# A fused two-block transformer forward on one core: a fourth weight slot in attention, another order in the last expert unit, unread products in three waits

## The chip, the cores and the metric

The kernel runs on one core of a Trainium2 chip. The metric is the device time of one execution in microseconds. The engines are named as in the profile: PE is TensorE (matmul), PEld its weight loads, DVE VectorE, ACT ScalarE, POOL GpSimd, and SP is the engine whose queue issues most of the DMA transfers. SBUF is the on-chip memory, and PSUM the small memory of eight banks into which TensorE writes. A bank holds 512 fp32 columns on 128 partitions.

## The reference

The sequence has 256 tokens, the model 1024 channels, and everything is fp32. The first block is one layer, cut here to what matters:

```
mod = silu(c) @ w_ada + b_ada                  # shifts, scales, gates
h   = rms_norm(x) * (1 + sc_mix) + sh_mix
u, v, tq, tk, tv, nq, nk, nv, ga, gb = split(h @ w_in + b_in)
o_a = u * (w_s applied to layer_norm(v) + tiny_attention(tq, tk, tv) @ tiny_w_o)
o_b = neighbourhood_attention(nq, nk, nv, context, rpb)       # 16 heads of 32
x   = x + g_mix * ((sigmoid(ga)*(o_a @ w_up_a) + sigmoid(gb)*(o_b @ w_up_b)) @ w_out)
h2  = rms_norm(x) * (1 + sc_ffn) + sh_ffn
y   = shared_swiglu(h2) + sum over the top 8 of 64 experts of weight * swiglu_e(h2)
x   = rms_norm(x + g_ffn * y) * final_norm_g
```

The second block is two layers of stick-breaking and block attention with gates, a SwiGLU feed-forward part and layer norms, on the first block's x. Weights are some 400 MB, which are read once.

## The kernel before

**Weights.** They are streamed as chunks of 128x2048 fp32 (1 MB) in one fixed order by the class `Ring`. `Ring.open(pool, n, limit)` gives it n slots of a pool; `_issue` asks for the next chunk by a DMA on SP (L222) or, where its number is in `halves`, by two DMAs of half a chunk. `done(i)` gives the slot of chunk i to the next chunk of the order. An expert's source is a function, since the expert's number is read at run time.

**Products.** Most products keep fp32 accuracy by a split: ACT casts a weight chunk to `whi` (L352), DVE subtracts to get `wlo` (L353), and TensorE makes three products in a fast fp32 format (L392 to L394). The split of a chunk is made ahead, into one of two buffers. Some small products are in full fp32, which TensorE does by two instructions each.

**Order of the work.** Instructions are put in order on each engine by a planner that simulates their times and takes the order in which they are written as priority; a semaphore is set wherever one engine reads what another wrote. `follow()` and `issue_after` hold TensorE to a written order.

**Start.** Each of the six parts of `mod` is made by `ada_group(g)`: products of silu(c) with chunks of w_ada (L701), then `end()` adds the bias (`row`, L708), then `fm()` transposes `row` (L714) and DVE copies it to `mod` (L719). The first group stands ahead of the modulated input `xT` (L844), its cast `hh` (L288) and rest `hl` (L289), which are the operands of the first in-projection.

**Attention stage** (183 to 279 us in the trace). `weave` mixes two lists: the main one has the in-projection chunks of the two gates (ga, gb), each chunk split and multiplied, with further w_ada chunks consumed by DVE between them (`gate`, L749); the other has eight steps of the spatial gating unit (`sgu`, L1245 to L1250) and the neighbourhood attention (`na`). The ring has three slots here. In `na`, for each of four head groups and two halves of the queries, TensorE makes scores (L1311), DVE adds the bias table T, ACT takes the exponentials P (L1265), TensorE transposes them (L1278), ACT copies them to a tile PT (L1279), and `av` multiplies by the values (L1344) and by the reciprocal of the sums: DVE takes the reciprocal of four sums per row, spread to 32 columns each (`rB`, L1335), TensorE transposes that (L1337), ACT copies it (`o`, L1340). PT has two buffers; the gating unit's constants (`tw`) lie in one of them.

**Experts.** Experts sit in 26 units of one, two or four experts which share 128 rows; the last unit has four, with 32 rows each. For a unit TensorE gathers its tokens, multiplies by gate and up (L1627), ACT and DVE form the activation, TensorE transposes it to `aT` (L1656), and `down(p, h)` multiplies by the down chunks for each half h of the output columns: for f in two halves of the inner dimension, for e in the experts, with expert e in column tile e of the array (L1666). DVE multiplies by the gate (`yf`, L1763), ACT and DVE split the result into `yh` and `yl` (L1764, L1765), and `comb` adds it to the tokens' sums by four products for each of the two (L1679).

**Final.** `a(t)` makes the sums of squares (ACT, L1879) and the normed `xr` (DVE, L1885); `b` transposes it (L1931) and splits it for the second block.

Of the kernel before, what the change touches and what calls it, by code (L numbers as in the profile page):

```python
# [9 lines left out]
F32 = mybir.dt.float32  # L10
# [4 lines left out]
OP = mybir.AluOpType  # L15
# [6 lines left out]
SLOT = 2048  # L22
# [10 lines left out]
UNITS = [(2, 0), (2, 2), (2, 4), (2, 6)]  # L33
# [146 lines left out]
class Ring:  # L180
# [29 lines left out]
    def _issue(self, pool):  # L210
        if pool.name in self.lasting and self.wait_from <= self.next < self.wait_to:

            self.held.append(pool)
        elif self.next < self.limit[pool.name]:
            t = pool.tile([128, SLOT], F32, tag="w", name="w")
            src = self.src[self.next]
            if self.next in self.halves:
                for h in range(2):
                    s = slice(h * SLOT // 2, (h + 1) * SLOT // 2)
                    self.nc.sync.dma_start(t[:, s], src[:, s])  # L220
            else:
                self.last = self.nc.sync.dma_start(t[:], src() if callable(src) else src)  # L222
            self.tiles[self.next] = t
            self.home[self.next] = pool
            self.next += 1
            if self.next == self.stop:
                self.wait_from, self.wait_to = self.stop + self.EARLY, math.inf
                self.free()
# [43 lines left out]
class Kernel:  # L272
# [38 lines left out]
    @contextmanager  # L311
    def follow(self):

        traced = self.nc.cur_bb.bb.instructions
        n = len(traced)
        with self.tc.issue_after(self.pe_last) if self.pe_last else ExitStack():
            yield
        for i in traced[n:]:
            if i.engine == mybir.EngineType.PE:
                self.pe_last = i  # L320

    def last(self, engine):
        return next(i for i in reversed(self.nc.cur_bb.bb.instructions) if i.engine == engine)
# [244 lines left out]
    def program(self):  # L568
        tc, nc, A = self.tc, self.nc, self.A
        with ExitStack() as es:  # L570
# [66 lines left out]
            self.ring.add(order)  # L637
            self.ring.stop = self.ring.wait_to = self.i_2[0][0]
            self.ring.wait_from = self.ring.stop - self.KEEP
            self.ring.halves = (self.i_ada[3], self.i_uv[0])  # L640
            self.setup()
            self.block1()
            self.block2()
# [46 lines left out]
    def ada_group(self, g):  # L690
        nc = self.nc
        st = {}

        def begin():
            st["ps"] = self.accp.tile([128, 512], F32, tag="acc", name="acc")

        def step(k):
            i = self.i_ada[4 * g + k // 2]
            w = self.ring.get(i)[:].rearrange("p (k c) -> p k c", k=2)
            for j in range(4):  # L700
                nc.tensor.matmul(st["ps"][32 * j:32 * j + 32, 0:256], self.silp[:, k, :], w[:, k % 2, j * 256:(j + 1) * 256],  # L701
                                 start=k == 0, stop=k == 7, tile_position=(0, 32 * j))
            if k % 2:
                self.ring.done(i)

        def end():
            row = self.prep.tile([128, 256], F32, tag="row", name="row")
            nc.vector.tensor_tensor(row[:], st["ps"][:, 0:256], self.bada[:, g], op=OP.add)  # L708
            st["row"] = row

        def fm():
            pt = self.accp.tile([128, 512], F32, tag="acc", name="acc")
            for h in range(2):
                nc.tensor.transpose(pt[:, h * 128:(h + 1) * 128], st["row"][:, h * 128:(h + 1) * 128], self.ident)  # L714
            src = pt[:, 0:256].rearrange("p (h j c) -> p h j c", h=2, c=32)
            for n in range(2):
                dst = self.mod[:, n, 4 * g:4 * g + 4].rearrange("p (j h) r -> p h j r", h=2)
                for r in range(2):
                    nc.vector.tensor_copy(dst[:, :, :, r], src[:, :, 2 * n:2 * n + 2, r])  # L719
            ks = slice(4 * g, 4 * g + 4)  # L720
            for r in range(2):
                nc.vector.scalar_tensor_tensor(self.a1[:, r, ks], self.mod[:, 1, ks, r], 1.0, self.vecs[:, V_NMG + 4 * g:V_NMG + 4 * g + 4],
                                               op0=OP.add, op1=OP.mult)

        return [begin] + [lambda k=k: step(k) for k in range(8)] + [end, fm]
# [56 lines left out]
    def block1(self):  # L782
# [227 lines left out]


        tmp, tmp_es = self.pool("atmp", "right", bufs=2)
        oah = op.tile([128, 8, 256], F32R, name="oah")
        oal = Parts()
        obh = op.tile([128, 4, 256], F32R, name="obh")
# [13 lines left out]
        self.weave(main, bg)  # L1029
        self.dump("oa", oah[:].bitcast(F32))  # L1030
        self.dump("ob", obh[:].bitcast(F32))
        tmp_es.close()
        att_es.close()
        xp, xp_es = self.pool("xp", "right")
# [196 lines left out]

    def sgu(self, tmp, tT, u, vn, oah, oal):
        nc, A = self.nc, self.A
        big = tmp.tile([128, 2048], F32, tag="PT", name="tw")
        two, bs, wst = big[0:64, 0:1024], big[64:65, 0:1024], big[:, 1024:2048]
        nc.sync.dma_start(two, A["two"])
        nc.sync.dma_start(bs, A["bs"])
        nc.sync.dma_start(wst, A["wst"])
        ones1 = self.ones[64:65, :]

        def sgu(g):
            ps = self.accp.tile([128, 512], F32, tag="acc", name="acc")
            o = ps[:, 0:256]
            gs = slice(g * 128, (g + 1) * 128)
            nc.tensor.matmul(o, two[:, gs], tT[:], start=True, stop=False, skip_group_check=True)  # L1245
            nc.tensor.matmul(o, ones1, bs[:, None, gs].to_broadcast([1, 2, 128]), start=False, stop=False, skip_group_check=True)
            for n in range(2):
                nc.tensor.matmul(ps[:, n * 128:(n + 1) * 128], vn[:, n, gs], wst[:, gs], start=False, stop=n == 1,
                                 skip_group_check=True)
            nc.vector.tensor_tensor(o, u[g][:], o, op=OP.mult)  # L1250
            u[g] = None
            lo = self.up.tile([128, 256], F32R, tag="u", name="oal", bufs=9)
            oal.parts.append(lo)
            self.split(o, oah[:, g], lo[:])

        return [lambda g=g: sgu(g) for g in range(8)]
# [24 lines left out]
    def na(self, ap, tmp, qd, kd, nv, obh, obl):  # L1281
        nc, A, c = self.nc, self.A, self.c
        st = {}
# [40 lines left out]

        def trp(g, q, j):
            if j == 0:
                st["PT", g, q] = tmp.tile([128, 4, 4, 128], F32, tag="PT", name="PT")
            self.transposeP(st.pop(("p", g, q, j)), st["PT", g, q][:, :, j, :], 4)

        def av(g, q):  # L1330
# [1 line left out]
            r = st.pop(("r", g, q))  # L1332
            ps = self.accp.tile([128, 512], F32, tag="acc", name="acc")
            rB = tmp.tile([128, 4, 32], F32, tag="obf", name="rB")
            nc.vector.reciprocal(rB[:], r[:, :, None].to_broadcast([128, 4, 32]))  # L1335

            nc.tensor.matmul(ps[:, 128:256], rB[:].rearrange("p a b -> p (a b)"), self.ident, start=True, stop=False,  # L1337
                             skip_group_check=True)
# [214 lines left out]
    def moe(self, xnh, xnl, gf, h2, after, mmes, ranks, overflow):  # L1553
# [97 lines left out]
        def tra(p):  # L1651
# [4 lines left out]
            nc.vector.tensor_copy(aT[:], ps[:, 0:256])  # L1656
            st["aT"] = aT

        def down(p, h):
            y = self.bank(pg, "y")  # L1660
            n = UNITS[p][0]
# [84 lines left out]
            nc.gpsimd.dma_start(t[:], bass.AP(tensor=r.tensor, offset=r.offset + R_FG + h * 512, ap=[[0, 128], [1, 512]]))  # L1746
            self.fg.append(t)
        comb(nu - 2)
        down(nu - 1, 0)
        down(nu - 1, 1)  # L1750
        comb(nu - 1)
        self.overflow_loop(pg, xnh, xnl, [xgs[0][:].rearrange("p a b -> p (a b)"), wx[0][:], wx[1][:], xgs[1][:, :, 0:64]], gf)
        self.ring.go_on()
        mp_es.close()
# [105 lines left out]
    def final(self, fp):  # L1860
# [29 lines left out]

        a(0)
        a(1)
        self.pieces = 4
        b(0)
        self.open_hlx(0)
# [505 lines left out]
```

## Time and profile before

| | |
|---|---|
| median of 3 runs | 1612.58 us (1611.51 to 1612.89) |
| the profiled execution's own time | 1612.77 us |
| its span | 1611.0 us |
| mean granted clock of TensorE | 0.99 |
| TensorE, DVE, ACT busy | 97%, 55%, 39% of the span |
| instructions | 26016 |

The span goes from the first to the last instruction; the rest of the own time lies around it. A busy share is of the whole span; the stages differ, so the rows below are taken stretch by stretch. The granted clock is in parts of full speed: 1.00 is 2.4 GHz and 0.50 is 1.2 GHz. In rows of waits the instruction that waited is named first, then the one that it waited for.

### The profile page before, as it was taken

What the parts mean: (1) busy time and instruction counts of PE and PEld (TensorE: products, weight loads), DVE (VectorE), ACT (ScalarE), POOL (GpSimd) and SP (SyncE); (2) the same over time, 40 slices, a digit from 0 to 9 for tenths busy, and PEclk for the clock granted to TensorE, in tenths of its full rate; (3) what the DMA queues carried; (4) which work ended last, traced back from release to release, by engine and by line L of the source; (5) the groups of instructions that cost most, each with busy time, mean ns of one, the idle gap of its engine ahead of it and who ended that gap; (6) DMA issues with size and microseconds to landing.
All of it is one profiled execution on the core that took longest, in us unless ns stands there. A gap on an engine that the chain in (4) does not pass through costs nothing. (4 is left out here: it accounts for less than half of the span.)

```text
span 1611.0 us, 26016 instructions
## 1 busy us (share of the span) xinstructions
PE 1557.7 (97%) x10509; PEld 1204.2 (75%) x10509; DVE 878.6 (55%) x1639; ACT 632.3 (39%) x1171; POOL 12.8 (1%) x23
## 2 busy tenths in 40 slices
PE   6999988999999999999989999999999999999997
PEld 4799876975443444443349999899999999899996
DVE  3696697663332323332344667964446565975453
ACT  3633366442111111111134756554433656644440
POOL 0000000000000000000000000000000000000000
PEclk9999999999999999999999999999999999999999
DMA  9788586878999999999955446565552444756530
GB/s 369 267 312 273 154 229 196 332 296 343 397 421 420 421 420 421 421 420 420 422 231 191 154 139 213 199 235 185 184 181 79 157 158 137 250 215 209 184 131 27
DMA packets 62972, 419.48 MB, mean 260 GB/s; under 512 B 7393, under 2 KB 9057, under 8 KB 14210
## 3 DMA queue, kind: packets, MB, share of 16 engines
q1 hardware_dynamic: 59010, 408.63, 67.7%
q0 software_dynamic: 1088, 5.61, 1.0%
q10 hardware_dynamic: 2752, 3.55, 0.6%
q8 instruction: 83, 1.36, 0.3%
q14 instruction: 39, 0.32, 0.1%
HBM read 413.05 MB, written 4.19 MB: 259 GB/s over the span
## 5 line engine op out<-in xcount | busy, mean ns | idle before, releaser
L353 DVE TENSOR_TENSOR wlo<-w,whi 128x1024 fp32r<-128x1024 f32 (+1 forms) x384 | 374.9, 1014 | 171.2 <-ACT whi L352 168.7
L352 ACT CAST whi<-w 128x1024 fp32r<-128x1024 f32 (+1 forms) x384 | 319.2, 883 | 316.9 <-PE mm L393 140.1
L392 PE MATMUL mm<-xTh,whi 128*128 128x256 f32 x960 | 274.5, 286 | 0.0
L394 PE MATMUL mm<-xTh,wlo 128*128 128x256 f32 x960 | 271.5, 283 | 0.0
L393 PE MATMUL mm<-xTl,whi 128*128 128x256 f32 x960 | 271.0, 282 | 0.0
L1627 PE MATMUL gu<-w,xg 128*64 128x512 f32 (+2 forms) x936 | 207.0, 596 | 0.0
L392 PEld LDWEIGHTS mm<-xTh,whi 128*128 128x128 f32 x960 | 182.9, 191 | 2.2 <-issue 1.4
L393 PEld LDWEIGHTS mm<-xTl,whi 128*128 128x128 f32 x960 | 183.4, 191 | 0.6
L394 PEld LDWEIGHTS mm<-xTh,wlo 128*128 128x128 f32 x960 | 182.8, 190 | 0.0
L1627 PEld LDWEIGHTS gu<-w,xg 128*64 128x64 f32 (+2 forms) x936 | 58.7, 127 | 98.5 <-issue 93.7
L1666 PE MATMUL y<-w,aT 128*64 128x512 f32 (+2 forms) x432 | 114.4, 599 | 0.0
L1648 DVE SCALAR_TENSOR_TENSOR sil<-sil,wsl,gu 128x256 f32<-128x256 f32 x26 | 12.5, 481 | 128.2 <-ACT sil L1647 127.6
L1764 ACT CAST yh<-yf 128x512 fp32r<-128x512 f32 x52 | 32.2, 619 | 125.9 <-DVE yf L1763 125.9
L392 PE MATMUL mm<-hh,whi 128*128 128x256 f32 x256 | 76.1, 299 | 5.6 <-ACT whi L352 3.9
L1763 DVE TENSOR_TENSOR yf<-y,gf 128x512 f32<-128x512 f32 x52 | 35.9, 690 | 79.4 <-PE y L1666 79.4
L394 PE MATMUL mm<-hh,wlo 128*128 128x256 f32 x256 | 75.0, 295 | 2.9 <-DVE wlo L353 2.9
L1666 PEld LDWEIGHTS y<-w,aT 128*64 128x64 f32 (+2 forms) x432 | 32.7, 126 | 57.5 <-issue 55.4
L393 PE MATMUL mm<-hl,whi 128*128 128x256 f32 x256 | 74.9, 294 | 0.3 <-DVE hl L289 0.3
L484 PE MATMUL acc<-whi,xTh 128*128 128x256 f32 x256 | 73.8, 289 | 0.0
L485 PE MATMUL acc<-wlo,xTh 128*128 128x256 f32 x256 | 72.6, 285 | 0.0
L486 PE MATMUL acc<-whi,xTl 128*128 128x256 f32 x256 | 72.4, 286 | 0.1
L1647 ACT ACTIVATE sil<-gu 128x256 f32<-128x256 f32 x26 | 10.0, 383 | 134.3 <-PE gu L1627 134.3
(449 smaller groups left out, 3119.9 us busy)
## 6 DMA issues: line engine op xcount, KB each, us to landing
w<-in_we SPq DMA_DIRECT2D x171, 1024.0 KB, 19.8
w<-in_w SPq DMA_DIRECT2D x156, 1024.0 KB, 4.9
w<-in_wada SPq DMA_DIRECT2D x23, 1024.0 KB, 8.9
wx<-in_we SPq DMA_DIRECT2D x21, 1024.0 KB, 19.8
ks<-kd SPq DMA_DIRECT2D x8, 512.0 KB, 7.3
lngb<-in_rows POOLq DMA_DIRECT2D x4, 1024.0 KB, 5.2
T<-in_rpb SPq DMA_DIRECT2D x8, 384.0 KB, 7.9
qs<-qd SPq DMA_DIRECT2D x16, 128.0 KB, 8.3
```

What stands on the lines that cost most here:

```text
L352: nc.scalar.copy(hi[:, s], w[:, s])
L353: self.lo_of[i] = nc.vector.tensor_tensor(lo[:, s], w[:, s], hi[:, s].bitcast(F32), op=OP.subtract)
L392: nc.tensor.matmul(ps, hi[:, k, mm], h, start=first, stop=False, skip_group_check=True)
L393: nc.tensor.matmul(ps, hi[:, k, mm], l, start=False, stop=False, skip_group_check=True)
L394: nc.tensor.matmul(ps, lo[:, k, mm], h, start=False, stop=last, skip_group_check=True)
L484: nc.tensor.matmul(o, h, wh, start=k == 0 and c % 2 == 0, stop=False, skip_group_check=True)
L485: nc.tensor.matmul(o, h, wl, start=False, stop=False, skip_group_check=True)
L486: nc.tensor.matmul(o, l, wh, start=False, stop=k == 7 and c % 2 == 1, skip_group_check=True)
L1627: nc.tensor.matmul(st["gu"][m * e:m * e + m, :], xg[:, k, s0:s0 + m], w[:, k % 4, :], start=k == 0, stop=k == 7, tile_position=(0, m * e))
L1666: nc.tensor.matmul(y[m * e:m * e + m, :], st["aT"][:, f * 128 + e * m:f * 128 + e * m + m], w[:, f, h * 512:(h + 1) * 512], start=f == 0, ...
L1763: nc.vector.tensor_tensor(t[0:n], y[0:n], g[0:n, h * 512:(h + 1) * 512], op=OP.mult)
L1764: nc.scalar.copy(yh[0:n], t[0:n])
```

## The change

In five parts, as in the diff:

1. `Ring._issue` can load a chunk whose source is a function by two halves, and the last down chunk of the last expert unit is added to `halves`.
2. `idle(ps, n)` makes n products of the identity with itself that nobody reads. Four are put behind the last product of the first ada group (columns 256 to 383 of the bank that `row` reads), seven behind its transposes (the same columns of the bank that `mod` reads), and one plus twelve between `a` and `b` of the final norm, into a bank of their own.
3. The attention stage gets a pool `extn` of one weight slot, opened at its start and closed at its end. The tiles with tag PT (`tw` and PT) have one buffer instead of two.
4. In `av`, DVE takes the reciprocal of the four sums in place and then copies it to the 128x128 tile.
5. For the last expert unit `down_last` takes the products expert by expert (for e, for f, for h; chained in that order), keeps `yf` whole in fp32, and `comb_last` adds it by four full fp32 products instead of eight in the fast format.

```diff
-            if self.next in self.halves:
+            if self.next in self.halves and not callable(src):
...
+            elif self.next in self.halves:
+                src = src()
                 for h in range(2):
                     s = slice(h * SLOT // 2, (h + 1) * SLOT // 2)
                     self.nc.sync.dma_start(t[:, s], src[:, s])
...
+    def idle(self, ps, n):
+        for _ in range(n):
+            self.nc.tensor.matmul(ps, self.ident, self.ident, start=False, stop=False, skip_group_check=True)
...
-            self.ring.halves = (self.i_ada[3], self.i_uv[0])
+            self.ring.halves = (self.i_ada[3], self.i_uv[0], self.i_d[-1][-1])
...
         def end():
+            if g == 0:
+                with self.tc.issue_after(self.last(mybir.EngineType.PE)):
+                    self.idle(st["ps"][:, 256:384], 4)
...
+            if g == 0:
+                with self.tc.issue_after(self.last(mybir.EngineType.PE)):
+                    self.idle(pt[:, 256:384], 7)
...
         tmp, tmp_es = self.pool("atmp", "right", bufs=2)
+        extn, extn_es = self.pool("extn", "right")
+        self.ring.open(extn, 1, self.i_upa[0])
...
+        extn_es.close()
         tmp_es.close()
...
-        big = tmp.tile([128, 2048], F32, tag="PT", name="tw")
+        big = tmp.tile([128, 2048], F32, tag="PT", name="tw", bufs=1)
...
-                st["PT", g, q] = tmp.tile([128, 4, 4, 128], F32, tag="PT", name="PT")
+                st["PT", g, q] = tmp.tile([128, 4, 4, 128], F32, tag="PT", name="PT", bufs=1)
...
-            nc.vector.reciprocal(rB[:], r[:, :, None].to_broadcast([128, 4, 32]))
+            nc.vector.reciprocal(r[:], r[:])
+            nc.vector.tensor_copy(rB[:], r[:, :, None].to_broadcast([128, 4, 32]))
...
+        def down_last(p):
+            n = UNITS[p][0]
+            m = 128 // n
+            ys = [self.bank(pg, "y") for _ in range(2)]
+            for e in range(n):
+                w = self.ring.get(self.i_d[p][e])[:].rearrange("p (k c) -> p k c", k=2)
+                for f in range(2):
+                    for h in range(2):
+                        with self.follow():
+                            nc.tensor.matmul(ys[h][m * e:m * e + m, :], st["aT"][:, f * 128 + e * m:f * 128 + e * m + m],
+                                             w[:, f, h * 512:(h + 1) * 512], start=f == 0, stop=f == 1, tile_position=(0, m * e))
+            for i in self.i_d[p]:
+                self.ring.done(i)
+            for h in range(2):
+                t = self.xp.tile([128, 512], F32, tag="x1%d" % h, name="yf")
+                nc.vector.tensor_tensor(t[:], ys[h][:], gf[:, h * 512:(h + 1) * 512], op=OP.mult)
+                st["y", p, h] = t
+
+        def comb_last(p):
+            ST = st.pop(("ST", p))[0]
+            ys = [st.pop(("y", p, h)) for h in range(2)]
+            for t in range(2):
+                for h in range(2):
+                    nc.tensor.matmul(self.acc[t][h][:], ST[:, t * 128:(t + 1) * 128].bitcast(F32), ys[h][:],
+                                     start=False, stop=False, skip_group_check=True)
...
         comb(nu - 2)
-        down(nu - 1, 0)
-        down(nu - 1, 1)
-        comb(nu - 1)
+        self.pe_last = None
+        down_last(nu - 1)
+        comb_last(nu - 1)
...
         a(0)
         a(1)
+        ps = self.mmp.tile([128, 512], F32, tag="mm", name="mm")
+        nc.tensor.matmul(ps[:, 0:128], self.ident, self.ident, start=True, stop=False, skip_group_check=True)
+        self.idle(ps[:, 0:128], 12)
```

## Rows read from the trace of the kernel before

**Rows 1.** The page: span, and busy time (share of the span) xinstructions by engine.
```profile
span 1611.0 us, 26016 instructions
...
PE 1557.7 (97%) x10509; PEld 1204.2 (75%) x10509; DVE 878.6 (55%) x1639; ACT 632.3 (39%) x1171; POOL 12.8 (1%) x23
```

**Rows 2.** Windows: stretch, length, busy PE PEld DVE ACT POOL, granted clock, DMA, GB/s.
```profile
21.55:28.38 6.83, 5.84 (x25) 5.55 (x26) 6.83 (x16) 4.58 (x10) 0.00 (x0) 0.50 1.02 420
45.00:50.00 5.00, 4.89 (x28) 4.17 (x28) 4.56 (x15) 3.58 (x9) 0.00 (x0) 1.00 0.00 0
171.70:175.10 3.40, 3.40 (x17) 1.99 (x15) 2.27 (x4) 2.94 (x5) 0.00 (x0) 1.00 0.95 206
175.00:182.00 7.00, 7.00 (x25) 5.13 (x24) 3.65 (x7) 0.95 (x3) 0.00 (x0) 0.51 0.46 159
183.00:279.00 96.00, 83.44 (x741) 71.24 (x739) 83.52 (x117) 61.47 (x139) 2.77 (x5) 0.96 0.63 185
745.20:748.60 3.40, 3.40 (x16) 0.78 (x16) 0.48 (x1) 0.38 (x1) 0.00 (x0) 1.00 1.01 422
837.30:840.70 3.40, 3.28 (x16) 2.98 (x15) 3.40 (x11) 3.40 (x10) 0.00 (x0) 0.50 0.00 0
```

**Rows 3.** Waits of TensorE, 183 to 279 us: total, times, longest.
```profile
PE mm L392 <- ACT whi L352: 3.4, 2, 1.9
PE mm L394 <- DVE wlo L353: 1.9, 3, 0.8
```

**Rows 4.** Waits of TensorE, 835 us to the end, the two largest.
```profile
PE mm L1931 <- DVE xr L1885: 4.4, 1, 4.4
PE acc L2247 <- DVE qkT L2157: 0.4, 2, 0.2
```

**Rows 5.** Timeline at the start: begin, duration, engine, line [idle before it <- releaser].
```profile
19.70 0.42 DVE L708 TENSOR_TENSOR row<-acc,bada 128x256 f32<-128x256 f32 x1 [8.70 <-DMA w<-in_w]
...
20.72 0.37 DVE L719 COPY mod<-acc 128x4 f32<-128x4 f32 x4 [0.59 <-PE acc L714]
...
22.23 0.79 PE L392 MATMUL mm<-hh,whi 128*128 128x256 f32 x2 [1.55 <-ACT hh L288]
```

**Rows 6.** Timeline: fp32 products of 128 columns one after the other.
```profile
163.47 1.50 PE L1248 MATMUL acc<-tw,v 128*128 128x128 f32 x12
```

**Rows 7.** Line L1344: its products (ns least, median, most), and a wait.
```profile
L1344 PE MATMUL acc<-PT,nv x256: 272/273/298, 200.6 to 281.0; 128*32 128x128 f32 x128
...
  ACT o L1340: 1.6, 5
```

**Rows 8.** Waits of SP's queue, 183 to 279 us.
```profile
SPq L222 <- DVE gate L749: 19.9, 4, 7.5
```

**Rows 9.** Groups by line, 183 to 279 us: busy us, mean ns | idle before.
```profile
L1279 ACT COPY PT<-acc 128x512 f32<-128x512 f32 x32 | 18.3, 589 | 12.6 <-PE acc L1278 12.6
...
L1335 DVE RECIPROCAL rB<-rs 128x128 f32<-128x128 f32 x8 | 7.5, 942 | 1.2 <-ACT P L1265 1.2
```

**Rows 10.** Timeline: two small operations of DVE.
```profile
7.82 0.16 DVE L306 TENSOR_TENSOR rs_w<-rs_y 128x2 f32<-128x2 f32 x1
...
68.32 0.22 DVE L687 CAST ub<-cst 128x128 bf16<-128x128 f32 x1
```

**Rows 11.** Timeline: the down products of two units with four experts, and what follows.
```profile
745.89 1.90 PE L1666 MATMUL y<-w,aT 128*32 128x512 f32 x4
...
821.81 0.42 DVE L1656 COPY aT<-misc 128x256 f32<-128x256 f32 x1
...
823.07 1.04 PE L1666 MATMUL y<-w,aT 128*32 128x512 f32 x2
...
...
824.71 3.67 PE L1666 MATMUL y<-w,aT 128*32 128x512 f32 x30
...
828.42 0.69 DVE L1763 TENSOR_TENSOR yf<-y,gf 128x512 f32<-128x512 f32 x1 [0.18 <-PE y L1666]
...
830.79 0.63 PE L1679 MATMUL acc<-yl,ST 128*128 128x512 f32 x2
```

More of the change, by code (lines that the diff above doesn't have):

```diff
@@ L216, in _issue @@
             src = self.src[self.next]
-            if self.next in self.halves:
+            if self.next in self.halves and not callable(src):
+                for h in range(2):
+                    s = slice(h * SLOT // 2, (h + 1) * SLOT // 2)
+                    self.nc.sync.dma_start(t[:, s], src[:, s])
+            elif self.next in self.halves:
+                src = src()
                 for h in range(2):
@@ L1657, in tra @@
             st["aT"] = aT
+        def down_last(p):
[19 more added lines that the diff above has]
+            for t in range(2):
+                for h in range(2):
+                    nc.tensor.matmul(self.acc[t][h][:], ST[:, t * 128:(t + 1) * 128].bitcast(F32), ys[h][:],
+                                     start=False, stop=False, skip_group_check=True)
         def down(p, h):
```

## Prediction

> **What bounds the kernel now.** I read the page first, then the table of windows, the waits of TensorE (PE) stretch by stretch, the groups by line where an engine is full, and the timeline at the three places that are edited. The page gives a span of 1611.0 us with TensorE busy in 97% of it and VectorE (DVE) in 55% [rows 1], so in the mean a microsecond comes off only where TensorE has less to do or waits less. The edits lie in four stretches, and each has its own limit.
>
> At the start, from 21.55 to 28.38 us, DVE is busy in all 6.83 us, the DMA engines are full, and TensorE is granted 0.50, which is 1.2 GHz of its two levels 1.2 and 2.4 [rows 2]. Later, from 45 to 50 us, the DMA stands at 0.00 while TensorE is busy in 4.89 of 5: the transfers wait for slots there, so what is lost or won before 45 us stays. In the attention stage, 183 to 279 us, TensorE has 83.44 and DVE 83.52 busy in 96 us at a mean clock of 0.96, and the DMA is at 0.63 [rows 2]. So neither bandwidth nor one engine alone is the limit; the two engines wait for each other. The waits of TensorE there begin with 3.4 us on whi and 1.9 on wlo, the split halves of the next weight chunk [rows 3]. Behind 835 us the waits of TensorE are one of 4.4 us (the final norm) and next to it 0.4 [rows 4]: the second block is bound by TensorE, so a shift at 835 us reaches the end whole.
>
> **The change part by part.** All is counted on the profiled execution, 1612.77 us (1611.0 of span and 1.77 around it), which lies 0.19 above the median of the runs shown, 1612.58.
>
> *Unread products at the start.* Four go between the last product of the first ada group and the DVE addition `row` (L708), seven between the transposes and the copies `mod` (L719) [rows 5]. A product in full fp32 is two instructions; twelve of them with 128 columns take 1.50 us [rows 6], 0.125 each. So 8 × 0.125 = 1.0 us stand before `row` and 14 × 0.125 = 1.75 before `mod`, if the readers wait for them. They write columns 256 to 383 of a bank of which only columns 0 to 255 are read, but the trace has this case: L1344 writes columns 0 to 127 of a bank and waited five times, 1.6 us in all, for ACT's copy `o`, which reads columns 128 to 255 of it [rows 7]. So I take it that they wait. `row` to `hh` is a chain (row, transposes, mod, a, xT, hh): it ends in the 1.55 us that TensorE waits for `hh` [rows 5], and DVE has no gap behind it [rows 2], so at worst the whole 2.75 us come out late. Against that, TensorE would stay at 2.4 GHz in the 6.83 us of half clock and could regain up to half of them, 3.4. The ends are 2.75 − 3.4 = −0.65 and +2.75. I take about the middle, +1.1: the lower end would need a DVE with time to spare, the upper a clock that TensorE could make no use of.
> The Trainium skill (PSUM — Partial Sum Buffer, "PSUM bank collisions raise a hardware error") says that accesses of two engines to PSUM are to be kept apart by bank and quadrant of partitions, not by address. L1344's waits agree with it; by this rule the products delay their readers (the sum above), and by a rule of addresses this term would be −0.65 and the total 1.75 lower.
>
> *The fourth slot.* SP waits with ring transfers for DVE's ada step `gate` (L749), 19.9 us in four, up to 7.5 [rows 8]: the next but one chunk is asked for only when a slot comes free in the midst of the chunk before it, so it lands late, its split comes late, and TensorE waits for whi. With one more slot the transfer is asked for a chunk earlier. What goes is the 3.4 us on whi; beyond them at most the 1.9 on wlo, and what the two spells of low clock cost, (1 − 0.96) × 96 = 3.8 us. I take −3.4, since wlo waits behind DVE, which stays nearly full. Late next is the softmax's P, for which DVE's reciprocal already waits 1.2 us [rows 9]. The slot is paid for by one PT tile instead of two: ACT's copies into it wait for the products that read the last one. Those copies follow the transposes (ACT is idle 12.6 us before them for that reason [rows 9]), and the products of the group before are then out, so I cost it at nothing; without that cover it is about one product of L1344, 0.27 us [rows 7], at each of 7 changes, 1.9 us. The slot's first transfer also stands in SP's queue ahead of the loads of tw, qs and the bias table T; one chunk of 1.05 MB at the 422 GB/s of a full window [rows 2] is 2.5 us, the worst that these could come later.
>
> *The reciprocal.* Eight on 128x128 take 0.942 us each [rows 9]. In their place stand one on 128x4 and a copy that spreads it. The nearest rows are a 128x2 DVE operation of 0.16 and a 128x128 cast of 0.22 [rows 10]: 0.942 − 0.38 = 0.56, times 8 = 4.5 us of DVE. DVE is busy 83.52/96 = 87% of the stage, so I put 0.87 × 4.5 = 3.9 on the path. Attention together: −3.4 − 3.9 = −7.3. The ends are −(3.4 + 1.9 + 3.8 + 4.5) = −13.6 and +1.9 + 2.5 = +4.4 (all cover gone and nothing gained).
>
> *The last expert unit.* Before, the down products of its four experts go to four column tiles side by side: two instructions from 823.07, and from 824.71 thirty in 3.67 us; the result is complete 0.18 before 828.42, at 828.24 [rows 11]. `aT`, which they need, is there at 821.81 + 0.42 = 822.23 [rows 11], and none of the 32 shows a wait for a DMA. So loading the last chunk by halves hides nothing: 0. But the new order takes one expert after the other: all eight instructions (four products) of one column tile, then those of the next. Where one tile worked alone, four took 1.90 us [rows 11], 0.475 each with the last one's end, so about 0.45 apart: 32 × 0.45 = 14.4, less one pitch of overlap at each of three changes of tile, 13.05. With one pair of the combination of the unit before among them, 0.63 as the last pair takes, they end at 823.07 + 0.63 + 13.05 = 836.75: +8.5. Then, before: from 828.24 to the end of the last combining products, 830.79 + 0.63 = 831.42, are 3.18 us. After: 0.18 of hand-over, 0.69 for the second `yf`, 0.1 and six fp32 instructions of 512 columns at 0.45 = 2.7, 3.67 (two of the eight run beside `yf`): +0.5. The cast to yh and the subtraction to yl, gone from that path, are counted in it. Tail: +9.0. The ends are 0 (the tiles overlap in this order too) and the doubled case below.
>
> *Unread products before the final norm.* 13 calls, 26 × 0.125 = 3.25 us, into a bank that nobody reads, inside a wait of 4.4 [rows 4]: they delay nothing. TensorE would be at 2.4 GHz where it is now at 0.50; but from 837.30 to 840.70 DVE and ACT are busy in all 3.40 us [rows 2]. I take −0.3, between 0 and half of that window, −1.7.
>
> Sum: +1.1 − 7.3 + 9.0 − 0.3 = +2.5, so 1612.77 + 2.5 = 1615.3 us.
>
> **The rivals.**
> *The clock falls in the tail* (slower). Only a quarter of the array's columns works at a time there. For it: from 171.70 to 175.10 TensorE is busy in all 3.40 us, with products that use few rows, and then runs at 0.51 from 175 to 182 [rows 2]. Against it: 745.20 to 748.60, which has the one-tile stretch, is at 1.00, though only half of it was one tile. It decides from the point where half of the 32 run at 1.2 GHz: 16 × 0.45 = 7.2 more, and 6 × 0.45 = 2.7 for the combination: 1615.3 + 9.9 = 1625.2.
> By the Trainium skill (TensorE: Matmul & The Clock Gate, Part 1) how busy TensorE has lately been sets its clock; by that alone the busy tail stays at 2.4 GHz and the sum stands, but the stretch from 171.70 speaks against busy time alone.
>
> *The new order costs nothing* (faster). The four experts' products don't depend on each other, and if TensorE starts a later tile's while the earlier is streaming, as it does for interleaved ones, the tail's 9.0 go: 1606.3. Against it, four of one tile in 1.90. The same side is reached if attention gains its whole 13.6: 1615.3 − 6.3 = 1609.0.
>
> *The slot isn't filled earlier* (slower): its transfer waits for memory, or DVE alone is the limit. Then attention gives 3.9 or less, 1615.3 + 3.4 = 1618.7; and 1624.5 where it gives nothing and the start costs its 2.75.
>
> **How the numbers follow.** A difference under 0.2%, 3.2 us, can't be told from none. The forecast has 0.42, within 1609 to 1620: 0.05 of that faster, 0.20 same, 0.17 slower. The falling clock has 0.30, all but 0.01 of it slower. The free order, or the whole gain in attention, has 0.20, of which 0.19 faster and 0.01 same. The slot that isn't filled has 0.08, slower but for 0.01. Together: faster 0.24, same 0.23, slower 0.53; I shift 0.04 of slower to faster, since attention's floor was worked out less surely than its ceiling. The predicted time is that of the likeliest. The range leaves out about 0.1 on each side: down to 1603 (the free order with some more in attention) and up to 1628 (the low clock with the start's upper end).
>
> **What would show it.** In the profile after: `row` and `mod` later by 1.0 and 2.75 with the clock at 1.00 around 25 us (start); no wait on whi over 1 us and a stage of attention shorter by 7 (slot); L1335's reciprocal under 0.2 us; the 32 down products of the last unit in some 13 us instead of 5, one column tile at a time (tail); the clock at 1.00 at 838 us. It is wrong if the stretch from `aT` of the last unit to the end of the combination stays near 9 us, or if it takes over 22; and if the stage of attention takes as long as before.

## The result, and the profile after

The changed kernel takes 1622.47 us (median of 4 runs, 1620.7 to 1623.14), the kernel before, timed beside it, 1612.74 (4 runs, 1611.51 to 1614.49). The ratio is 1.0057 with a 95% interval of 1.0045 to 1.0069: 9.2 us slower, 7.3 to 11.1. The profiled execution is the fastest of the four, 1620.7 us, with a span of 1618.9. It is 7.9 us above the span of before, and that is the difference which the traces explain.

The page of the changed kernel, the same two lines as in [rows 1]:

```profile
span 1618.9 us, 26125 instructions
...
PE 1568.4 (97%) x10557; PEld 1208.2 (75%) x10557; DVE 874.0 (54%) x1645; ACT 632.8 (39%) x1169; POOL 12.8 (1%) x23
```

TensorE is busy 10.7 us longer and DVE 4.6 us shorter. To see where the span grew I set TensorE's instructions of the two traces beside each other, line by line, and took how much later each stands (the median over 10 us). At 30 to 44 us it is 0.3 to 0.0; at 50 us 3.8; at 140 us 3.6; behind attention, at 280 us, 2.5; through all the experts 2.2 to 2.6; behind 840 us 8.0, and that to the end. So there are three steps: +3.6 at 45 to 50 us, −1.1 in attention, +5.4 between the last expert unit and the final norm.

**The start.** The timeline of the changed kernel at the places of [rows 5]:

```profile
19.48 1.16 PE L330 MATMUL acc<-cst 128*128 128x128 f32 x8
...
20.68 0.42 DVE L721 TENSOR_TENSOR row<-acc,bada 128x256 f32<-128x256 f32 x1 [8.29 <-PE acc L330]
...
21.49 1.73 PE L330 MATMUL acc<-cst 128*128 128x128 f32 x14
23.26 0.37 DVE L735 COPY mod<-acc 128x4 f32<-128x4 f32 x4 [0.35 <-PE acc L330]
...
25.30 0.91 PE L402 MATMUL mm<-hh,whi 128*128 128x256 f32 x3 [2.08 <-ACT hh L293]
...
44.45 0.42 DVE L721 TENSOR_TENSOR row<-acc,bada 128x256 f32<-128x256 f32 x1 [8.06 <-PE acc L711]
...
45.41 0.17 DVE L735 COPY mod<-acc 128x4 f32<-128x4 f32 x1 [0.53 <-PE acc L727]
...
45.48 2.50 DVE L363 TENSOR_TENSOR wlo<-w,whi 128x512 fp32r<-128x512 f32 x4
...
47.90 0.30 DVE L735 COPY mod<-acc 128x4 f32<-128x4 f32 x3
...
50.47 0.74 PE L402 MATMUL mm<-hh,whi 128*128 128x256 f32 x4 [2.35 <-ACT hh L293]
```

`row` and `mod` name TensorE's unread products (L330) as what they waited for; they begin 1.0 and 2.5 us later, and the first product with hh 3.1 us later. But at 40 us nothing is left of that: the clock is now 1.00 where it was 0.50 (first row below), and TensorE catches up. That it is the clock is borne out by kernel 8 below, which has the same products at the start but a spell at 1.2 GHz from 27.28 to 30.70 us: it is still 2.1 us late at 36 to 44 us. The loss comes at the second ada group, which holds no unread product. DVE's order has changed there: four pieces of wlo, 2.50 us, stand between the first `mod` copy and the other three, so `hh` is late and TensorE waits 2.35 us for it. Before, the four copies stood together and the wlo behind the chain:

```profile
45.44 0.37 DVE L719 COPY mod<-acc 128x4 f32<-128x4 f32 x4 [0.53 <-PE acc L714]
...
47.60 2.49 DVE L353 TENSOR_TENSOR wlo<-w,whi 128x512 fp32r<-128x512 f32 x4
...
48.01 0.28 PE L392 MATMUL mm<-hh,whi 128*128 128x256 f32 x1
```

The windows of the changed kernel (columns as in [rows 2]); 187 to 283 us is its attention stage, 825.7 to 835.2 the down products of the last unit:

```profile
21.55:28.38 6.83, 4.73 (x38) 4.33 (x38) 6.47 (x19) 4.43 (x10) 0.00 (x0) 1.00 1.01 419
45.00:50.00 5.00, 3.12 (x14) 2.28 (x14) 4.59 (x14) 2.07 (x4) 0.00 (x0) 1.00 0.22 36
...
187.00:283.00 96.00, 85.40 (x749) 72.14 (x748) 79.37 (x124) 61.97 (x138) 2.77 (x5) 0.94 0.65 190
825.70:835.20 9.50, 9.50 (x35) 2.59 (x34) 0.69 (x1) 0.00 (x0) 0.00 (x0) 1.00 0.10 42
```

**Attention.** DVE has 79.37 us of work in place of 83.52, 4.2 less where 4.5 were worked out, but the mean clock is 0.94 in place of 0.96. The waits of TensorE in 187 to 283 us, for [rows 3]:

```profile
PE mm L404 <- DVE wlo L363: 2.5, 3, 1.0
PE acc L1357 <- DVE rB L1355: 2.5, 1, 2.5
PE acc L1330 <- ACT P L1284: 1.6, 3, 1.0
PE mm L402 <- ACT whi L362: 1.4, 3, 0.9
```

The wait on whi fell from 3.4 to 1.4 and none is over 0.9; a wait of 2.5 on rB stands in its place, and wlo has 2.5 where it had 1.9.

**The tail.** The timeline of the last unit, for [rows 11], and of the final norm behind it:

```profile
825.69 1.04 PE L1689 MATMUL y<-w,aT 128*32 128x512 f32 x2
...
827.32 8.00 PE L1689 MATMUL y<-w,aT 128*32 128x512 f32 x30
...
835.26 3.70 PE L1704 MATMUL acc<-yf,ST 128*128 128x512 f32 x8
...
841.10 0.49 PE L1942 MATMUL mm<-cst 128*128 128x128 f32 x2 [2.14 <-DVE rs_a L303]
...
841.42 2.84 PE L330 MATMUL mm<-cst 128*128 128x128 f32 x24
...
842.52 1.41 DVE L1933 SCALAR_TENSOR_TENSOR xr<-acc,rs_y,fg 128x512 f32<-128x512 f32 x2
...
844.10 1.04 PE L1982 MATMUL mm<-cst,xr 128*128 128x128 f32 x8
```

The thirty products took 8.00 us in place of 3.67: 4.3 more. In the trace one by one, most come in pairs, and the pairs 0.43 us apart; the first four and the last four come singly. By the written order, eight for each expert, the last four of an expert so run beside the first four of the next: two column tiles work where four did. The eight full fp32 combining products end at 838.96. From `aT` (824.42) that is 14.5 us, before 831.42 − 821.81 = 9.6: +4.9, of which 0.6 is the whole fp32 result. Then the unread products begin 2.14 us into the wait and not at its start. They end at 844.26, behind `xr`, and the transposes begin 1.6 us after xr's start (844.10 − 842.52) where they began 0.8 after it (835.80 − 834.99). Before:

```profile
834.99 1.41 DVE L1885 SCALAR_TENSOR_TENSOR xr<-acc,rs_y,fg 128x512 f32<-128x512 f32 x2
...
835.80 1.97 PE L1931 MATMUL mm<-cst,xr 128*128 128x128 f32 x8 [4.37 <-DVE xr L1885]
```

### The profile page after: what moved, and what is told of

It is laid out like the page before. It is cut to its first block, busy times and chain, and to the rows that moved or that the text cites. A ratio compares the mean times of both kernels' runs of the same rounds, so it can differ in the third digit from the quotient of the medians.

```text
span 1618.9 us, 26125 instructions
## 1 busy us (share of the span) xinstructions
PE 1568.4 (97%) x10557; PEld 1208.2 (75%) x10557; DVE 874.0 (54%) x1645; ACT 632.8 (39%) x1169; POOL 12.8 (1%) x23
## 5 line engine op out<-in xcount | busy, mean ns | idle before, releaser
L1714 PE MATMUL y<-w,aT 128*64 128x512 f32 (+2 forms) x400 | 109.8, 599 | 0.0
## 6 DMA issues: line engine op xcount, KB each, us to landing
T<-in_rpb SPq DMA_DIRECT2D x8, 384.0 KB, 10.1
```

What stands on the lines that cost most here:

```text
L1714: nc.tensor.matmul(y[m * e:m * e + m, :], st["aT"][:, f * 128 + e * m:f * 128 + e * m + m], w[:, f, h * 512:(h + 1) * 512], start=f == 0, ...
```

## The experiments

Times are against the kernel before on the same chip. Three groups of four kernels were timed, with 17, 29 and 23 runs of the kernel before (medians 1611.22, 1611.81 and 1611.10); ratios with 95% intervals. "Later" is TensorE's lateness against the trace of before, found as above, of one profiled execution each. Between 280 and 800 us, where no edit lies, the kernels gain up to 2.3 us on the trace of before (the changed one nothing): at 503 us it waits 1.1 us for an expert's weights, the changed kernel 0.8, kernels 1, 5, 8 and 12 not at all. So a part of the change is best read over its own stretch. "Half clock" is the time at 1.2 GHz between 140 and 290 us in that execution.

| kernel | median us | ratio | later at 100, 280, 900 us | half clock us |
|---|---|---|---|---|
| before | 1611.1 to 1612.7 | 1 | 0, 0, 0 | 13.7 |
| after | 1622.47 | 1.0057 [1.0045, 1.0069] | 3.9, 2.5, 8.0 | 20.5 |
| 1 no products at the start | 1614.59 | 1.0020 [1.0011, 1.0029] | −0.3, −1.4, 3.6 | 13.7 |
| 2 these in their own bank | 1617.67 | 1.0034 [1.0021, 1.0047] | 0.8, 2.2, 7.8 | 27.3 |
| 3 last unit as before | 1616.57 | 1.0035 [1.0022, 1.0048] | 3.9, 5.9, 4.4 | 27.3 |
| 4 last unit interleaved | 1618.28 | 1.0043 [1.0030, 1.0056] | 3.9, 2.7, 4.2 | 20.5 |
| 5 before + slot | 1608.58 | 0.9983 [0.9975, 0.9992] | −0.3, −4.7, −5.7 | 10.2 |
| 6 before + reciprocal | 1612.30 | 1.0001 [0.9992, 1.0010] | −0.1, 0.1, −0.5 | 10.2 |
| 7 before + both | 1609.44 | 0.9984 [0.9975, 0.9992] | −0.5, −1.5, −1.4 | 23.9 |
| 8 no final products | 1620.12 | 1.0050 [1.0037, 1.0062] | 4.2, 1.6, 5.4 | 13.7 |
| 9 before, reciprocal twice | 1610.69 | 0.9999 [0.9987, 1.0010] | 0.1, −2.4, −3.4 | 10.2 |
| 10 only the seven at the start | 1623.55 | 1.0071 [1.0055, 1.0086] | 4.9, 5.1, 10.1 | 23.9 |
| 11 only the four at the start | 1621.06 | 1.0054 [1.0038, 1.0070] | 3.9, 2.6, 8.4 | 20.5 |
| 12 slot, early final products | 1608.71 | 0.9982 [0.9970, 0.9994] | −1.4, −3.0, −4.9 | 17.1 |

**1. Without the products at the start.**

```diff
-            if g == 0:
-                with self.tc.issue_after(self.last(mybir.EngineType.PE)):
-                    self.idle(st["ps"][:, 256:384], 4)
...
-            if g == 0:
-                with self.tc.issue_after(self.last(mybir.EngineType.PE)):
-                    self.idle(pt[:, 256:384], 7)
```

> The changed kernel without the eleven unread products at the start. Theory (the trace after): they share a bank with row and mod, so these wait, DVE's planned order puts 2.5 us of wlo in the midst of the next group's mod copies at 45 us, and TensorE is 3.6 us late from 48 us on. Then DVE's order is that of before, TensorE is within 0.3 us of before at 50 to 160 us, and the time is 1622.5 - 3.6 = 1618.9. Rival (the lateness at 48 us comes from something else, as the next chunk's earlier transfer): it stays 3.6 late there, 1622.5.

The timeline of this kernel at the second ada group:

```profile
45.09 0.37 DVE L729 COPY mod<-acc 128x4 f32<-128x4 f32 x4 [0.53 <-PE acc L724]
...
47.26 2.49 DVE L363 TENSOR_TENSOR wlo<-w,whi 128x512 fp32r<-128x512 f32 x4
...
47.66 0.28 PE L402 MATMUL mm<-hh,whi 128*128 128x256 f32 x1
```

The four copies are together again, wlo stands behind the whole chain (47.26 in place of 45.48), and the products with hh begin at 47.66 in place of 50.47. TensorE is 0.3 us early up to 100 us. In time it is 6.0 us less than the changed kernel (0.0037 × 1612); with both intervals that is 3.5 to 8.4, so it agrees with the 3.9 that the traces show at 280 us (2.5 + 1.4); the 3.6 expected lie at the lower end. The theory stands.

**2. The same products in a bank of their own.**

```diff
-                    self.idle(st["ps"][:, 256:384], 4)
+                    self.idle(self.spare(), 4)
...
-                    self.idle(pt[:, 256:384], 7)
+                    self.idle(self.spare(), 7)
...
+    def spare(self):
+        ps = self.mmp.tile([128, 512], F32, tag="mm", name="mm")
+        self.nc.tensor.matmul(ps[:, 0:128], self.ident, self.ident, start=True, stop=False, skip_group_check=True)
+        return ps[:, 0:128]
```

> The changed kernel with the start's unread products (one more each time) in a bank that nobody reads. Theory: row begins at 19.7 and mod at 20.7 us as before, DVE's order is that of before, and the clock is 1.00 near 25 us; time 1618.9 as without the products, and up to 1.5 lower where the high clock lets u's first chunk end earlier. Rival (the price is TensorE's time for the products, not the shared bank): hh's product still begins near 25.3 us, 1622.5.

Half a hit: DVE's order is that of before and nothing is lost at 48 us, but TensorE is still 0.8 us late at 100 us. With no reader to wait for, the planner put some of these products in the midst of the ada products, and `row` began at 21.63 in place of 19.70. The first product with hh begins at 24.15, between the 22.23 of before and the 25.30 of the changed kernel. So what costs at 48 us goes with the readers' wait in the shared bank, not with the products as such. The clock is 1.00 near 25 us, and still this kernel is 1.1 us behind kernel 1. The time, 1.0034, is not lower than without the products.

**3. The last unit as before.**

```diff
-        self.pe_last = None
-        down_last(nu - 1)
-        comb_last(nu - 1)
+        down(nu - 1, 0)
+        down(nu - 1, 1)
+        comb(nu - 1)
...
-            self.ring.halves = (self.i_ada[3], self.i_uv[0], self.i_d[-1][-1])
+            self.ring.halves = (self.i_ada[3], self.i_uv[0])
```

> The changed kernel with the last expert unit as before (products interleaved over the four experts, split result, last chunk whole). Theory: 32 products again within 5.2 us instead of 9.5 and the combination 3.2 instead of 3.8 behind them: 1622.5 - 4.9 = 1617.6. Rival (loading by halves earns something that the order gives away): less, 1620.

```profile
828.61 3.67 PE L1714 MATMUL y<-w,aT 128*32 128x512 f32 x30
```

From 800 to 900 us this kernel loses 0.5 us, the changed one 5.4: the 4.9 expected. In time the part is 0.0022 × 1612 = 3.5, whose interval (0.7 to 6.4) holds 4.9. Loading by halves earned nothing that shows here.

**4. Only the order.**

```diff
-            for e in range(n):
-                w = self.ring.get(self.i_d[p][e])[:].rearrange("p (k c) -> p k c", k=2)
-                for f in range(2):
-                    for h in range(2):
+            for f in range(2):
+                for h in range(2):
+                    for e in range(n):
+                        w = self.ring.get(self.i_d[p][e])[:].rearrange("p (k c) -> p k c", k=2)
```

> The changed kernel with only the order of the last unit's products changed to f, h, expert, whole fp32 result kept. Theory (it is the order: neighbours of one column tile wait for each other): 30 products in 3.7 instead of 8.0 us, 1622.5 - 4.3 = 1618.2. Rival (the whole fp32 result is what costs): no more than 0.5 lower, 1622.

```profile
826.19 3.63 PE L1689 MATMUL y<-w,aT 128*32 128x512 f32 x30
829.79 3.70 PE L1704 MATMUL acc<-yf,ST 128*128 128x512 f32 x8
...
835.63 0.49 PE L1942 MATMUL mm<-cst 128*128 128x128 f32 x2 [2.14 <-DVE rs_a L303]
835.96 4.28 PE L330 MATMUL mm<-cst 128*128 128x128 f32 x24
...
840.03 1.28 PE L1982 MATMUL mm<-cst,xr 128*128 128x128 f32 x8
```

Thirty products in 3.63 us with the whole fp32 result kept: it is the order that costs, 4.4 us. In time it was 2.3 us less than the changed kernel (interval −0.6 to 5.1). In the profiled execution something else took back 1.7 (the tail lost 2.7 us from 800 to 900, where 5.4 − 4.4 = 1.0 would be left): the clock was half near 838 us, so the unread products took 4.28 us in place of 2.84 and the transposes began that much later.

**5 to 7. Slot and reciprocal alone and together, on the kernel before.**

```diff
+        extn, extn_es = self.pool("extn", "right")
+        self.ring.open(extn, 1, self.i_upa[0])
...
+        extn_es.close()
...
-        big = tmp.tile([128, 2048], F32, tag="PT", name="tw")
+        big = tmp.tile([128, 2048], F32, tag="PT", name="tw", bufs=1)
...
-                st["PT", g, q] = tmp.tile([128, 4, 4, 128], F32, tag="PT", name="PT")
+                st["PT", g, q] = tmp.tile([128, 4, 4, 128], F32, tag="PT", name="PT", bufs=1)
```

> The kernel before with the fourth weight slot of attention alone (one PT buffer). Theory (the five traces after: 140 to 280 us came out 2.1 shorter with 13.7 us of half clock, as in before, and 1.7 to 2.2 longer with 27.3): what is not waited for goes back through TensorE's clock; 0 to -1.5 us against before, with the waits on whi gone. Rival (the prediction's size): -3.4.

```diff
-            nc.vector.reciprocal(rB[:], r[:, :, None].to_broadcast([128, 4, 32]))
+            nc.vector.reciprocal(r[:], r[:])
+            nc.vector.tensor_copy(rB[:], r[:, :, None].to_broadcast([128, 4, 32]))
```

> The kernel before with the short reciprocal and the copy alone. Both theories: 8 x 0.56 = 4.5 us less of DVE. Theory (TensorE and its clock set the stage as much as DVE): 0 to -1.5 us. Rival (the prediction's size, DVE's share of the path): -3.9.

> The kernel before with slot and reciprocal together, nothing else of the change. Theory: -2 us where the spells of half clock in 140 to 290 us sum to 13.7 us as in before, 0.3 us more for each us of them more, so -2 to +2 from run to run. Rival (the prediction): -7.3.

The slot alone makes the kernel 2.7 us faster (interval 1.3 to 4.0): nearer to the prediction's 3.4 than to my theory's 0 to 1.5, of which the interval leaves only the end. Its wait of TensorE on whi, 183 to 279 us:

```profile
PE mm L392 <- ACT whi L352: 1.3, 3, 0.9
```

The wait on wlo (1.9 before) is gone from this trace, as from those of kernels 1, 2, 7 and 12; on P it waits 6.2 us where it waited 3.5. The price of the single PT buffer, which the prediction took at nothing, may be in 1.4 us of waits on ACT's copies PT (0.2 before, 0.2 in the changed kernel).

The reciprocal alone makes 0.2 us of difference, with an interval of −1.3 to 1.6 that leaves out the prediction's −3.9, and both together no more than the slot. It does what it says; the groups by line of kernel 6, and DVE's work there in the window 140 to 290 us (110.44 in the kernel before):

```profile
L1336 DVE COPY rB<-rs 128x128 f32<-128x128 f32 x8 | 1.8, 224 | 0.1
...
L1335 DVE RECIPROCAL rs<-rs 128x4 f32<-128x4 f32 x8 | 1.4, 172 | 2.2 <-ACT P L1265 2.2
```

```profile
140.00:290.00 150.00, 137.11 (x1103) 113.44 (x1102) 105.74 (x166) 81.73 (x173) 2.78 (x5) 0.97 0.69 209
```

DVE works 4.7 us less, and TensorE stands 0.1 us later at 280 us. DVE's idle time before the reciprocal grew from 1.2 [rows 9] to 2.2 us: some of what is saved is waited for at P. TensorE's waits change places: on wlo 3.2 us where it was 1.9, on whi 2.3 where it was 3.4.

**8. Without the final products.** The three lines behind `a(1)` are taken out.

> The changed kernel without the thirteen unread products before the final norm's transposes. Theory (they begin late, behind a wait for DVE, and end after xr is ready): the transposes begin 0.8 us after xr instead of 1.6 where the clock is high and 3.2 where it is half, so 0.5 to 2.1 us less than the changed kernel, which was 9.1 to 9.7 above before: +7 to +9. Rival (the prediction: they fit in the wait and win 0.3): +9.5 to +10.

1.0050 against 1.0057 is 1.1 us less, with an interval that holds 0 and 2.1: inconclusive in time. In the traces the changed kernel loses 5.4 us from 800 to 900, this one 5.2, with half clock from 839.66 to 846.48. So where the products kept the clock high they gave back about what they cost. They don't always keep it: near the final norm each of the six kernels without them (before, 5 to 9) has a spell of 6.8 us at 1.2 GHz, and of the eight with them four have none (after, 3, 10, 12) and four one of 3.4 us (1, 2, 4, 11).

**9. The long reciprocal twice.**

```diff
+            nc.vector.reciprocal(rB[:], r[:, :, None].to_broadcast([128, 4, 32]))
             nc.vector.reciprocal(rB[:], r[:, :, None].to_broadcast([128, 4, 32]))
```

> The kernel before with each of the eight long reciprocals made twice, so 8 x 0.94 = 7.5 us more of DVE in the attention stage. Theory (DVE's work in av lies beside TensorE's; the short reciprocal alone had made 0.0): -0.5 to +2 us. Rival (the prediction: 87% of DVE's time in the stage is on the path): +6.5.

The groups by line of this kernel and its window 140 to 290 us:

```profile
L1336 DVE RECIPROCAL rB<-rs 128x128 f32<-128x128 f32 x8 | 7.6, 945 | 0.1
L1335 DVE RECIPROCAL rB<-rs 128x128 f32<-128x128 f32 x8 | 7.5, 941 | 0.3 <-ACT P L1265 0.3
```

```profile
140.00:290.00 150.00, 137.45 (x1125) 116.17 (x1124) 117.19 (x166) 82.12 (x173) 2.78 (x5) 0.97 0.72 210
```

DVE works 117.19 us in place of 110.44, and the time is 0.9999 [0.9987, 1.0010]. The rival would have been 1.0040. So neither 4.7 us less nor 6.8 us more of DVE moves the kernel. It isn't that nobody waits for the longer work. TensorE's wait on rB, 183 to 279 us, in the kernel before, in kernel 6 and in this one:

```profile
PE acc L1337 <- DVE rB L1335: 0.8, 1, 0.8
...
PE acc L1338 <- DVE rB L1336: 0.5, 2, 0.3
...
PE acc L1338 <- DVE rB L1336: 3.7, 6, 1.0
```

But TensorE's listed waits of that stage add up to 12.1 us before, 12.7 in kernel 6 and 12.1 here: while the one on rB grows by 2.9, those on whi and wlo fall from 3.4 and 1.9 to 1.9 and 0.6. Why the sum holds was not settled.

**10 and 11. Only the seven, only the four at the start** (the other block of experiment 1 taken out).

> The changed kernel with only the seven unread products between the transposes and mod, without the four before row. Theory: mod still waits 1.75 us, DVE's planned order puts four pieces of wlo behind the next group's mod copies and ahead of xT, and TensorE waits about 2 us for hh near 48 us: 2 to 3.6 us above the changed kernel without either, so +5 to +7 against before. Rival (the four before row are what does it): +3.3 as without either.

> The changed kernel with only the four unread products before row. Theory: a delay of 1.0 is enough for the planner to put a split ahead of mod and, in the next group, wlo between row and mod, and TensorE is 2 to 3.6 us late from 48 us: +5 to +7 against before. Rival (the seven do it): +3.3.

Either is enough: 1.0071 and 1.0054, as slow as both. Kernel 10 at the second ada group:

```profile
45.05 0.37 DVE L732 COPY mod<-acc 128x4 f32<-128x4 f32 x4 [0.53 <-PE acc L724]
45.33 2.48 DVE L363 TENSOR_TENSOR wlo<-w,whi 128x512 fp32r<-128x512 f32 x4
...
50.10 0.73 PE L402 MATMUL mm<-hh,whi 128*128 128x256 f32 x4 [2.35 <-ACT hh L293]
```

Kernel 11, where the mod copies follow at 47.76:

```profile
45.36 2.48 DVE L363 TENSOR_TENSOR wlo<-w,whi 128x512 fp32r<-128x512 f32 x4
```

In each of the three kernels the wlo stands at another place in the chain (amid the copies, behind them, ahead of them), and each time TensorE waits 2.35 us for hh and is 3.6 to 4.9 us late from 50 us on. The times are above the expected +5 to +7.

**12. Slot, and the final products written first.**

```diff
+        ps = self.mmp.tile([128, 512], F32, tag="mm", name="mm")
+        nc.tensor.matmul(ps[:, 0:128], self.ident, self.ident, start=True, stop=False, skip_group_check=True)
+        self.idle(ps[:, 0:128], 12)
         a(0)
         a(1)
```

> The kernel before with the fourth slot, and with the thirteen unread products of the final norm written ahead of its first sum of squares. Theory: where they begin at the end of the combination they end 3 us later, ahead of xr, the transposes begin 0.8 after xr, and at the high clock up to 1 us is won: -3 to -4 against before (the slot alone made -2.7). Rival (they wait for the same step of DVE as behind the sums and delay the transposes by 0.8 to 2.4): -0.5 to -2.

```profile
828.19 0.49 PE L1900 MATMUL mm<-cst 128*128 128x128 f32 x2 [2.07 <-DVE rs_a L298]
828.51 2.84 PE L325 MATMUL mm<-cst 128*128 128x128 f32 x24
829.68 1.41 DVE L1893 SCALAR_TENSOR_TENSOR xr<-acc,rs_y,fg 128x512 f32<-128x512 f32 x2
831.19 1.04 PE L1942 MATMUL mm<-cst,xr 128*128 128x128 f32 x8
```

They began at the same step of DVE, 2.07 us late, and the transposes came 1.5 us after xr's start: the rival's mechanism. The time, 2.9 us faster than before, is that of the slot alone. What makes them wait for DVE there was not settled.

**The clock in attention.** Of the eleven kernels with the slot, the gain between 140 and 280 us goes with the half clock of the same execution: −4.4 us at 10.2 us (kernel 5), −2.1 and −2.3 at 13.7 (1 and 8), −1.4 at 17.1 (12), −1.0 to −1.1 at 20.5 (after, 4, 11), −0.8 and +0.4 at 23.9 (7, 10), +1.7 and +2.2 at 27.3 (2, 3). That is 0.37 us for each us of half clock (6.4 over 17.1). The three without the slot don't show it: 0 at 13.7 (before), +0.3 and −2.5 at 10.2 (6, 9). From run to run of one kernel it shows again: mean clock and span of all 176 runs, each kernel against its own mean, give 0.30 us for each us of half clock in the whole span, with a correlation of 0.72. Both are correlations; whether the spells cost the time or the waits bring the spells was not tested. Which spells come varies from kernel to kernel, so the slot's gain in one trace lies anywhere between +2 and −4.

The products at the start reach into this stage as well. In the six kernels that have them in the readers' bank (after, 3, 4, 8, 10, 11) DVE and TensorE take the stage's instructions in another order than in kernels 1, 2 and 7, and TensorE waits 2.5 to 2.6 us for wlo; in kernels 1, 2, 5, 7 and 12 it doesn't wait for wlo at all. In gain that doesn't show: at the same half clock both orders come out alike, −2.1 and −2.3 at 13.7 us (1 and 8), +1.7 and +2.2 at 27.3 (2 and 3).

## Why the prediction was right, and where it was not

The forecast was 1615.3 us, slower by 2.5 on the profiled execution; measured were 7.9 there and 9.2 by the ratio. The side and the range held. The central value was 7.2 low, and its terms were further off than their sum: the last unit came out 4.1 us cheaper than its term, and attention, start and final products 6.2, 2.5 and 0.8 dearer. That these are partly opposite is luck, and a range of 25 us is wide enough for it. Against the trace:

- **Start: +1.1 predicted, +3.6 found.** That readers wait for products in other columns of their bank was right, and its direct price too (row +1.0, mod +2.5). The high clock then won this back in full by 40 us, near the lower end of the bounds. What was missed is the step after it: with either block of products in the readers' bank the planner moved a 2.50 us split into the chain of the next group (experiments 1, 10 and 11), and the order of the attention stage changed too; with the products in a bank of their own neither happened (experiment 2). That it does so because of its own simulated times is argued, not shown. The sentence "The ends are 2.75 − 3.4 = −0.65 and +2.75" ended its view at the edited group.
- **Slot: −3.4 predicted, 2.7 faster measured alone.** Right in mechanism (whi 3.4 to 1.3 us) and nearly in size; in the trace of kernel 5 attention is 4.4 us shorter. That it frees nothing on wlo holds only beside the reordered start (2.5 to 2.6 us); in kernels 1, 2, 5, 7 and 12 this wait is gone.
- **Reciprocal: −3.9 predicted, 0 found.** This is the step that failed: "DVE is busy 83.52/96 = 87% of the stage, so I put 0.87 × 4.5 = 3.9 on the path". The size of the saving was right (4.7 us). A busy share doesn't say what an operation costs: with the reciprocal at less than half its length, and at twice its length, the kernel took the same time (experiments 6 and 9). A part is slack behind ACT's P (DVE's idle time there is 2.2 us with the short one, 1.2 before, 0.3 with two). The rest shows as waits of TensorE that change their line, while their sum stays at 12.1 to 12.7 us.
- **Attention in the change: −7.3 predicted, −1.1 found**, from the reciprocal's 3.9 that weren't there and, if the slope above is a price, 2.5 us for a longer half clock, 20.5 in place of 13.7 us. By the prediction's own sign, a stage that "takes as long as before", this part was close to wrong.
- **Last unit: +9.0 predicted, +4.9 found.** That the new order gives up column tiles beside each other, and that halves hide nothing, was right. The mis-sized term is "less one pitch of overlap at each of three changes of tile": the trace has four at each, so two tiles ran side by side for most of it, 9.6 us from the first product to the last and not 13. The combination's +0.5 measured 0.6. (The 828.24 read as the end of the thirty products is the end of the first `yf`; they end at 824.71 + 3.67 = 828.38, which moves 0.14 from one term to the other.)
- **Final products: −0.3 predicted, +0.5 found** (5.4 less the tail's 4.9). The step from "inside a wait of 4.4" to "they delay nothing" failed: 3.3 us of work fit into 4.4 only if it starts early in it, and it started 2.1 late. Kernels 1, 2 and 11 show it dearer with half clock, about +2.1 (7.0 from 800 to 900 us, less 4.9).

Of the rivals' times 1624.5 lies nearest (its terms, 2.75 + 9.0 − 0.3 on 1612.77, add up to 1624.2): attention gives nothing and the start costs its 2.75. The sizes came near, 1.1 and 3.6, but not the mechanism: the slot was filled in time, since whi fell to 1.4 and the slot alone gains 2.7. The next, the clock falling in the tail (1625.2), did not happen: the window from 825.70 has 1.00 throughout, with TensorE busy in all 9.50 us. By the Trainium skill (TensorE: Matmul & The Clock Gate, Part 1) a busy TensorE keeps its clock, and this tail agrees; the stretch from 171.70 [rows 2] remains the exception.

The parts as timed, against the changed kernel or before: start 6.0, last unit 3.5, final products 1.1, slot and reciprocal −2.6, together 8.0 of the 9.2; each is uncertain by 1 to 3 us. The best version run is the kernel before with the slot alone, 1608.58 us, 2.7 faster than before; with the reciprocal or the early final products added (7, 12) it can't be told apart from it.

## What to carry to other kernels

Don't take a share of an operation's time for its price: a busy share doesn't give it, and here neither shortening nor doubling moved the time. Doubling the operation on the chip tells it in one run; look at the waits as well, since a wait on it may only take the place of another. Where a planner orders the engines, a delay of 1 us in one place can go with another order in the next stages: compare each engine's order, not only the edited lines. Filler work on TensorE has to start when the wait starts, and in a bank that no one reads, or it becomes the wait.

## What the runs showed that I had not expected

Products given to TensorE expert by expert still ran two column tiles at a time: pairs 0.43 us apart, the last four of one tile with the first four of the next. And the kernel's spread from run to run (1608.7 to 1617.2 for the kernel before) is of the size of single edits: between 140 and 290 us the time at half clock differed between 10.2 and 27.3 us among kernels of nearly the same work, and among those with the slot 0.37 us of time went with each us of it.
